# A hybrid attention and mLSTM block: attention products of the second half of the queries in another bank, six weight tiles, the bias table head by head, gate products in four column groups

## The chip, the cores and the metric

The kernel runs on one core of a Trainium2 chip. The metric is the device time of one execution in microseconds, 1434.75 us as the median of three runs before the change (1434.04 to 1437.02). A core has engines that work beside each other: TensorE (matrix products), VectorE, ScalarE and GpSimd (element-wise work), SyncE (it issues transfers), and 16 DMA engines. Each executes its own instructions in order; semaphores tie them together. The profile calls them PE, DVE, ACT, POOL and SP; PEld is TensorE's loading of weights.

## The reference

One layer over x, 1024 tokens by 1024 channels:

```python
xn = _rmsnorm(h, norm_w[layer])
(da_q, da_k, da_v, da_z, ml_q, ml_k, ml_v, ml_o, ml_z, ml_i, ml_f,
 gate_a, gate_m) = [xn @ wp for wp in _split_columns(w_in[layer])]
y_a = _diff_attention(da_q, da_k, da_v, lam[layer], subln_w[layer], rel_bias,
                      lambda_init) * jax.nn.silu(da_z)
y_m = _mlstm(ml_q, ml_k, ml_v, ml_i, ml_f, ml_o, ...) * jax.nn.silu(ml_z)
merged = g_a * (y_a @ w_pa[layer]) + g_m * (y_m @ w_pm[layer])
h = h + merged @ w_out[layer]
```

The attention has 8 heads. For each block of 128 queries:

```python
bias = rel_bias[_rel_bucket(kpos[None, :] - qpos[:, None])]
mask = (kpos[None, :] // CHUNK) <= (qpos[:, None] // CHUNK)
logits = jnp.einsum("pbhqd,pbhkd->pbhqk", qb, k).astype(jnp.float32) + bias
probs = jax.nn.softmax(jnp.where(mask, logits, NEG_INF), axis=-1)
attn = probs[0] - lam * probs[1]
return jnp.einsum("bhqk,bhkv->bhqv", attn, v)
```

so there are two softmaxes per head (p = 0 and 1), a bias that depends only on the distance of key and query, and a norm of each head's output. `ml_i` and `ml_f` are 16 columns of `w_in`, the gates of the mLSTM's eight heads.

## The kernel before

**Products.** Activations and weights are split into two float16 parts, and each float32 product is made of three (hi*hi, hi*lo, lo*hi: L329 to L331 with weights stationary, L358 to L360 with activations stationary). A unit is a set of 256 weight columns: it is loaded in two halves of 4 x 256 columns (L226, tiles `wt`, pool of `WT` = 3), squared on ScalarE for a common scale (L245, in `prep`), its scale is found by a short chain on VectorE with a TensorE sum in it (`fnorm_finish`, L165, L135 to L139), and it is split on ScalarE (L257) and VectorE (L259) into tiles `wp`. `prep` is a generator; the main loop takes one step of it with each step of the running unit's products.

**Start.** `normed` and `startup` bring x into the transposed, normalised, split form X (eight tiles, from transposes L396 read by ScalarE at L398 and VectorE at L399). `tables` is woven into the second half of it: it computes the differential factor, and the bias table `tb` (8 heads x 384 distances, a one-hot product), which L432 writes to memory for all heads at once, 128 copies of each row at a pitch of 513, so that a read with pitch 512 (`strip`, L584) yields each query's shifted row. The first unit of attention (`c_aqk(0)`, queries and keys of head 0) runs meanwhile, and `if_proj` makes the gates' 16 columns: `wifp` (32 columns, 16 hi and 16 lo) is stationary, 1024 tokens in two halves `th` stream by, and the sums over hi and lo parts of X are added up in one accumulation of 16 products for each half (L468).

**The order of phases.** `phases` lists groups of units, each with a side generator whose steps are put between the products: for seven groups `attention(h, PLAN_A)` of head h beside the units of head h + 1 (`aqk`, then `avz`), for the next `attention(7, PLAN_C)` beside the gate units, then the mLSTM heads. A plan entry (slot, name) puts a piece at a slot of the products' steps.

**One head's attention.** q_i is the product of query block i with all its keys for p = 0, r_i does the same for p = 1 and then combines and transposes (`both`); QK stands for these products (L812). They go to `psb`, one buffer of two banks, which VectorE reads with the bias strip in `BB` added and the maximum taken (L822); ScalarE makes the exponential (L826), VectorE combines the two softmaxes (L832 to L837), ScalarE and VectorE split the result (L844, L845) and a transposing DMA on SP (L847) turns it into z, the stationary operand of v_i (L855 to L857), the product with the values. v_0 to v_3 fill one bank of `pvp`, v_4 to v_7 the next buffer of that tag, and `pvp` has one buffer. f_k takes the factor of the output norm of four blocks on GpSimd (L862 to L864), o_k reads the bank with it on VectorE (L870), t_k transposes the result. The other small products and transposes take banks of the tag `pmi`, which has two buffers. `BB` is filled from the strip by VectorE at the start of each head (L800).

Of the kernel before, what the change touches and what calls it, by code (L numbers as in the profile page):

```python
# [48 lines left out]
def block_kernel(ctx, tc, x, norm_w, w_in, lam, subln_w, rel_bias, conv_w, conv_b, b_if,  # L49
# [355 lines left out]
    tb_d = dram.tile([H, P * 513], F32, tag="tbd", name="tb_d")  # L405

    def tables():
        oh = R(shape=[NB, 384], p="oh")
# [17 lines left out]
        tb_ps = m_ps()  # L426
        te.matmul(tb_ps[:H, :384], rb, oh, start=True, stop=True)
        tb = R(shape=[H, 384], p="tb")
        v.tensor_copy(tb, tb_ps[:H, :384])
        v.tensor_scalar(tb, tb, tb[:, 0:1], None, op0=ALU.subtract)  # L430

        nc.sync.dma_start(tb_d.rearrange("h (q u) -> h q u", u=513)[:, :, :384],  # L432
                    tb.unsqueeze(1).to_broadcast([H, P, 384]))
        yield
# [13 lines left out]
    gif_d = dram.tile([32, S], F32, tag="gifd", name="gif_d")  # L448

    def if_proj():  # L450
# [12 lines left out]
        t = R(shape=[32, S], p="gif")  # L463
        for th in range(2):
            gps = m_ps()
            for i in range(KC):
                for k in range(2):
                    te.matmul(gps[:32, :], parts[:, i, :], x_src(i, th)[k], start=(i + k == 0),  # L468
                              stop=(i + k == KC))
# [1 line left out]
            s.activation(t[:, HS[th]], gps[:32, :], AF.Copy, scale=sig[:32, :])
# [101 lines left out]
    def c_aqk(h, w):  # L573
# [10 lines left out]
        nc.sync.dma_start(strip, tb_d[h, :P * 512].rearrange("(q u) -> q u", u=512)[:, 127:383])  # L584
# [10 lines left out]
        def post(cb, th, ap):  # L595
# [7 lines left out]
            if done[cb] == 2:  # L603
                for p in range(2):
                    src = x2[p * 64:p * 64 + 64]
                    for j in range(2):
                        if cb == 0:
                            nc.sync.dma_start(Q[j * 64:j * 64 + 64, p, :], src[:, j, :])
                        else:
                            nc.sync.dma_start(K[p][j * 64:j * 64 + 64, :, :], src)  # L610
        return None, post
# [276 lines left out]
    def mlstm(h):  # L888
# [333 lines left out]
```

## Time and profile before

| | us |
|---|---|
| median of three runs | 1434.75 (1434.04 to 1437.02) |
| the profiled execution, its own time | 1435.78 |
| its span from first to last instruction | 1433.9 |
| TensorE busy | 1380.6 |
| VectorE busy | 848.0 |
| ScalarE busy | 735.0 |
| GpSimd busy | 157.5 |
| mean granted TensorE clock | 0.995 |

The profile records one execution. A row of a group names line, engine, operation, output <- inputs by the program's names, the count, busy time and the mean length of one; behind it stands the idle time of the engine just before such instructions and what ended most of it. A row of the timeline gives start and length, and in brackets the idle time before it and what ended that. TensorE's instructions overlap in the pipeline: one with 512 columns is shown with 380 ns, but the next starts 0.216 us later, with 256 columns 0.109 us later.

### The profile page before, as it was taken

Reading aid. Unit: us, or ns where it says so; the run is one execution under the profiler, and the core shown is the slowest. Engines: PE = TensorE matmul, PEld = TensorE weight load, DVE = VectorE, ACT = ScalarE, POOL = GpSimd, SP = SyncE. Lnnn points to the kernel's source line nnn. Section 1 sums busy time; section 2 is a strip of 40 time slices with the busy share of each in tenths; the row PEclk is TensorE's granted clock in tenths of the full one; section 3 lists DMA queues with packets and bytes.
Section 4 is the critical chain, followed back from the end, with each engine's and each line's share of the span. In section 5 each row is a group of like instructions: output and inputs, shape, how many; then the busy total and the mean of one; then the engine's idle time right before and its main releaser. Section 6 shows DMA issues by size and latency. Waiting matters only on the chain.

```text
span 1433.9 us, 25050 instructions
## 1 busy us (share of the span) xinstructions
PE 1380.6 (96%) x9650; PEld 913.3 (64%) x9650; DVE 848.0 (59%) x2310; ACT 735.0 (51%) x1533; POOL 157.5 (11%) x215
## 2 busy tenths in 40 slices
PE   6989999999999999999999999999999999999997
PEld 3656575665756655444486787778769675444786
DVE  6276868677686756533445674775866564233633
ACT  7276556565566667832353444443435344644542
POOL 2001010010100100100102020220211200122004
PEclk9999999999999999999999999999999999999999
DMA  6456355463554645543321313231232135534303
GB/s 200 68 142 140 83 107 124 104 141 82 114 121 91 136 95 130 163 149 125 96 74 60 104 31 101 47 87 47 66 97 75 60 86 158 168 103 162 118 16 118
DMA packets 232585, 150.14 MB, mean 105 GB/s; under 512 B 117297, under 2 KB 209730, under 8 KB 232466
## 3 DMA queue, kind: packets, MB, share of 16 engines
q1 hardware_dynamic: 218450, 123.28, 35.0%
q10 hardware_dynamic: 14016, 25.27, 5.3%
q8 instruction: 75, 1.23, 0.3%
q14 instruction: 44, 0.36, 0.1%
HBM read 90.12 MB, written 18.55 MB: 76 GB/s over the span
## 4 chain that ended last, share of the span: by engine, by line
PE 77%; DVE 9%; ACT 4%; DMA 4%; POOL 3%; issue 3%; SPq 0%; POOLq 0%; DVEq 0%; ACTq 0%
PE pp L329 14%; PE pp L331 14%; PE pp L330 14%; PE pp L360 8%; PE pp L358 8%; PE pp L359 8%; PE psb L812 3%; DVE z L822 3%; DMA z<-z 2%; ACT z L826 1%; DMA qw<-rows_d 1%; DVE wp L259 1%; PE psb L908 1%; PE pvp L855 1%; DVE hl L600 1%
## 5 line engine op out<-in xcount | busy, mean ns | idle before, releaser
L358 PE MATMUL pp<-wp,X 128*128 128x256 f16 x1280 | 349.7, 273 | 0.0
L359 PE MATMUL pp<-wp,X 128*128 128x256 f16 x1280 | 349.7, 273 | 0.0
L360 PE MATMUL pp<-wp,X 128*128 128x256 f16 x1280 | 349.7, 273 | 0.0
L329 PE MATMUL pp<-X,wp 128*128 128x512 f16 x768 | 291.7, 380 | 0.3 <-ACT wp L257 0.3
L331 PE MATMUL pp<-X,wp 128*128 128x512 f16 x768 | 291.3, 379 | 0.6 <-DVE wp L259 0.6
L330 PE MATMUL pp<-X,wp 128*128 128x512 f16 x768 | 291.8, 380 | 0.0
L257 ACT ACTIVATE wp<-wt,sb 128x512 f16<-128x512 f32 x208 | 136.9, 711 | 105.4 <-DVE sb L138 70.6
L331 PEld LDWEIGHTS <-wp 128*128 128x128 f16 x1024 | 100.0, 98 | 119.7 <-DVE wp L259 1.2
L245 ACT ACTIVATE junk<-wt 128x1024 bf16<-128x1024 f32 x112 | 118.1, 1055 | 100.0 <-DMA wt<-in_w_in_dram 89.7
L329 PEld LDWEIGHTS <-wp 128*128 128x128 f16 x1024 | 100.2, 98 | 103.0 <-issue 1.7
L330 PEld LDWEIGHTS <-wp 128*128 128x128 f16 x1024 | 100.1, 98 | 97.1
L259 DVE SCALAR_TENSOR_TENSOR wp<-wt,sb,wp 128x512 f16<-128x512 f32 x208 | 150.5, 760 | 14.4 <-ACT wp L257 12.8
L359 PEld LDWEIGHTS <-X 128*128 128x128 f16 x1280 | 125.3, 98 | 18.4 <-issue 2.4
L358 PEld LDWEIGHTS <-X 128*128 128x128 f16 x1280 | 125.4, 98 | 16.8 <-issue 0.8
L360 PEld LDWEIGHTS <-X 128*128 128x128 f16 x1280 | 125.3, 98 | 14.6
L826 ACT ACTIVATE z<-z,mx 128x256 f32<-128x256 f32 (+7 forms) x128 | 99.0, 773 | 61.7 <-DVE mx L825 46.1
L822 DVE CUSTOM_DVE_ANT_0 z<-psb,BB,negc 128x256 f32<-128x256 f32 (+7 forms) x128 | 104.1, 813 | 19.7 <-PE psb L812 19.4
L331 PE MATMUL pp<-Y,wp 128*128 128x512 f16 x256 | 97.1, 379 | 0.0
L330 PE MATMUL pp<-Y,wp 128*128 128x512 f16 x256 | 97.1, 379 | 0.0
L329 PE MATMUL pp<-Y,wp 128*128 128x512 f16 x256 | 97.1, 379 | 0.0
L649 DVE SCALAR_TENSOR_TENSOR acc<-up,wcol,acc 128x512 f32<-128x512 f32 x96 | 78.0, 827 | 27.4 <-POOL acc L650 24.5
L812 PE MATMUL psb<-K,Q 128*128 128x512 f16 (+3 forms) x384 | 83.5, 326 | 7.8 <-DMA K<-hl 4.6
(245 smaller groups left out, 2012.1 us busy)
## 6 DMA issues: line engine op xcount, KB each, us to landing
wt<-in_w_in_dram SPq DMA_DIRECT2D x128, 256.0 KB, 3.4
wt<-in_w_in_dram SPq DMA_DIRECT2D x24, 512.0 KB, 3.9
K<-hl SPq DMA_DIRECT2D x32, 256.0 KB, 3.7
gate_d<-tg ACTq DMA_DIRECT2D x32, 256.0 KB, 2.2
xt<-in_x_dram SPq DMA_DIRECT2D x8, 512.0 KB, 5.2
Q<-hl SPq DMA_DIRECT2D x32, 128.0 KB, 2.4
wt<-in_w_pa_dram SPq DMA_DIRECT2D x8, 512.0 KB, 5.4
ft<-gate_d ACTq DMA_DIRECT2D x16, 256.0 KB, 2.8
```

Source lines behind the costliest of these rows:

```text
L245: s.activation(j, w.wt[k], AF.Square, accum_out=ss[:, k:k + 1])
L257: s.activation(dst[0], src, AF.Copy, scale=w.sb)
L259: v.scalar_tensor_tensor(dst[1], src, w.sb, dst[0], op0=ALU.mult, op1=ALU.subtract)
L329: te.matmul(ps, wh, xh, start=(start and i == 0), stop=False, **kw)
L330: te.matmul(ps, wh, xl, start=False, stop=False, **kw)
L331: te.matmul(ps, wl, xh, start=False, stop=(stop and i == n - 1), **kw)
L358: te.matmul(ps[:, o], xh[:, t], wh, start=i == 0, stop=False)
L359: te.matmul(ps[:, o], xh[:, t], wl, start=False, stop=False)
L360: te.matmul(ps[:, o], xl[:, t], wh, start=False, stop=i == KC - 1)
L812: te.matmul(sp[:, c:e], Q[:, p, i * P:(i + 1) * P], K[p][:, j, c:e], start=(j == 0), stop=(j == 1))
L822: v.tensor_tensor_reduce(z[:, :n], sp[:, :n], bb[:, S - n:], negc, BIG, op0=ALU.add, op1=ALU.min, accum_out=mx)
L826: s.activation(z[:, :n], z[:, :n], AF.Exp, bias=mx, scale=-1.0, accum_out=rr[:, 2 * i + p:2 * i + p + 1])
```

## The change

The small products of the second half of the queries (v_4 to v_7) take a bank of the tag `pmi` instead of a new buffer of `pvp`, and `PLAN_A` puts v6, v7, f1 and o1 at other slots. The pool of weight tiles has six instead of three, the loads run one unit further ahead, and the third unit is loaded at the start. The bias table is written one head at a time on ScalarE's queue (`write_table`): head 0 from `tb` in a generator of its own (`first_table`), which also stores the 8 x 384 table, and each later head from that copy, a unit ahead of its use. The strip is read when the second column block of its unit is done (`bias_strip`), behind the issue of K, and the mask is made from the strip itself by one operation, without the constant `maskv`. The gate products of hi and lo and of the two halves go to four groups of 32 columns, in one bank of `psb`, issued in turn, and `if_gates` adds the parts up with two more loads and two more additions. The number of idle steps in `prep` becomes a parameter (5; 2 for the first unit), and the buffer `st` of the mLSTM has one copy.

The lists of `PLAN_A` are cut at their front:

```diff
-PLAN_A = [... (30, 'f0'), (30, 'o0'), (31, 'v6'), (31, 'v7'), (42, 't0'), (55, 'f1'), (55, 'o1'), (55, 't1')]
+PLAN_A = [... (30, 'f0'), (30, 'o0'), (33, 'v6'), (35, 'v7'), (42, 't0'), (43, 'f1'), (44, 'o1'), (55, 't1')]
-WT = 3
+WT = 6
...
+    s.dma_start(rb, rel_bias)
+    s.dma_start(oh, onehot)
...
+        for _ in range(slack):
+            yield
...
-    tb_d = dram.tile([H, P * 513], F32, tag="tbd", name="tb_d")
+    tb_d = [dram.tile([1, P * 513], F32, tag=f"tbd{h}", name=f"tb_d{h}") for h in range(H)]
+    tbr_d = dram.tile([H, 384], F32, tag="tbrd", name="tbr_d")
+
+    def write_table(h):
+
+        s.dma_start(tb_d[h].rearrange("h (q u) -> h q u", u=513)[:, :, :384],
+                    (tbr_d if h else tb)[h:h + 1].unsqueeze(1).to_broadcast([1, P, 384]))
+
+    def first_table():
+        for _ in range(3):
+            yield
+        tb_ps = m_ps()
+        te.matmul(tb_ps[:H, :384], rb, oh, start=True, stop=True)
+        tn0 = sm(p="tn0", bufs=1)
+        v.tensor_scalar(tn0[:H, :], tb_ps[:H, 0:1], -1.0, None, op0=ALU.mult)
+        s.activation(tb, tb_ps[:H, :384], AF.Identity, bias=tn0[:H, :])
+        yield
+        write_table(0)
+        s.dma_start(tbr_d, tb)
+        yield
 
...
-        nc.sync.dma_start(tb_d.rearrange("h (q u) -> h q u", u=513)[:, :, :384],
-                    tb.unsqueeze(1).to_broadcast([H, P, 384]))
...
-        t = R(shape=[32, S], p="gif")
-        for th in range(2):
-            gps = m_ps()
-            for i in range(KC):
+
+        t = R(shape=[P, 512], p="gif")
+        gps = s_ps()[:, :512]
+        for i in range(KC):
+            for th in range(2):
                 for k in range(2):
-                    te.matmul(gps[:32, :], parts[:, i, :], x_src(i, th)[k], start=(i + k == 0),
-                              stop=(i + k == KC))
-                yield
-            s.activation(t[:, HS[th]], gps[:32, :], AF.Copy, scale=sig[:32, :])
-        nc.sync.dma_start(gif_d, t)
+                    o = (th * 2 + k) * 32
+                    te.matmul(gps[o:o + 32, :], parts[:, i, :], x_src(i, th)[k], start=(i == 0), stop=(i == KC - 1))
+        yield
+        s.activation(t, gps, AF.Copy, scale=sig)
+        s.dma_start(gif_d, t)
...
+        for k, dst in ((0, gi), (1, ff), (2, gl[0]), (3, gl[1]), (4, gl[2]), (5, gl[3])):
+            r = k * H if k < 4 else 32 + (k - 4) * H
+            nc.sync.dma_start(dst.rearrange("h (t a) b -> h t (a b)", t=2),
+                              gif_d.rearrange("(t r) c -> r t c", t=2)[r:r + H])
...
+            v.tensor_tensor(dst, dst, gl[2 + k], op=ALU.add)
...
-        nc.sync.dma_start(strip, tb_d[h, :P * 512].rearrange("(q u) -> q u", u=512)[:, 127:383])
-        g.tensor_scalar(strip, strip, invc, 1.0, op0=ALU.mult, op1=ALU.mult)
         mc = sm(p="mc")
-        v.tensor_scalar(mc, invc, 2.0 ** 20, None, op0=ALU.min)
-        g.tensor_scalar(strip[0:64, 192:256], maskv, mc[0:64, :], 1.0, op0=ALU.mult, op1=ALU.mult)
+        v.tensor_scalar(mc, invc, 2.0 ** 20, -(2.0 ** 100), op0=ALU.min, op1=ALU.mult)
+        if h + 1 < H:
+            write_table(h + 1)
+
+        def bias_strip():
+            nc.sync.dma_start(strip, tb_d[h][0, :P * 512].rearrange("(q u) -> q u", u=512)[:, 127:383])
+            g.tensor_scalar(strip, strip, invc, 1.0, op0=ALU.mult, op1=ALU.mult)
+            masked = strip[0:64, 192:256]
+            g.tensor_scalar(masked, masked, 0.0, mc[0:64, :], op0=ALU.mult, op1=ALU.add)
...
+                if cb == 1:
+                    bias_strip()
...
-                ops[i // 4] = v_ps()
+                ops[i // 4] = m_ps() if i else v_ps()
...
+    order[2].finish_load()
...
-    weave(startup(1), tables())
+    weave(startup(1), tables(), first_table())
...
-                        pq[at + 1].start_load()
+                        pq[at + 1].finish_load()
+                    if at + 2 < len(pq):
+                        pq[at + 2].start_load()
```

What the scheduler makes of it is read from the order of the instructions. Numbers behind an underscore tell buffers apart; a line of after is that of before plus 1 to 21 (L329 to L331 are L330 to L332, L358 to L360 are L359 to L361, L812 is L833, L855 is L876, L870 is L891, L399 is L400); a bracket names the engines or DMA queues whose semaphores an instruction waits for.

First TensorE at v4 of head 2, before:

```order
L360 MATMUL pp_2844<-wp_2627,X_288 128x256
L358 LDWEIGHTS X_306
L358 MATMUL pp_2844<-wp_2642,X_306 128x256
L855 LDWEIGHTS z_2619 [waits DMAHW0_49]
L855 MATMUL pvp_2871<-vr_2064,z_2619 128x128 [waits DVE_49]
L856 LDWEIGHTS z_2619
```

and now:

```order
L360 MATMUL pp_2857<-wp_2646,X_271 128x256
L361 LDWEIGHTS X_271
L361 MATMUL pp_2857<-wp_2646,X_271 128x256
L876 LDWEIGHTS z_2628 [waits DMAHW7_49]
L876 MATMUL pmi_2884<-vr_2076,z_2628 128x128
L877 LDWEIGHTS z_2628
```

The product v4 goes to another bank, and its first matrix product waits for no engine any more, only its weight load for the transposed z. It stands 48 rows behind the head's last QK, with v3 among them; before it was 90, without v3.

Second TensorE where the QK of head 1 begin, at the end of head 0's phase. Before:

```order
L812 MATMUL psb_1697<-K_913,Q_912 128x128 [waits DMAHW0_49]
L812 LDWEIGHTS Q_912
L812 MATMUL psb_1697<-K_913,Q_912 128x128
L329 LDWEIGHTS wp_1474
L329 MATMUL pp_1689<-X_214,wp_1474 128x512
L330 LDWEIGHTS wp_1474
L330 MATMUL pp_1689<-X_214,wp_1474 128x512
L331 LDWEIGHTS wp_1474
L331 MATMUL pp_1689<-X_214,wp_1474 128x512
L812 LDWEIGHTS Q_912 [waits DMAHW3_49,DMAHW6_49,DMAHW4_49]
L812 MATMUL psb_1705<-K_914,Q_912 128x128 [waits DVE_49]
```

and now:

```order
L833 MATMUL psb_1714<-K_922,Q_920 128x128 [waits DVE_49]
L833 LDWEIGHTS Q_920
L833 MATMUL psb_1714<-K_922,Q_920 128x128
L833 LDWEIGHTS Q_920
L833 MATMUL psb_1727<-K_921,Q_920 128x256 [waits DVE_49]
L833 LDWEIGHTS Q_920
L833 MATMUL psb_1727<-K_921,Q_920 128x256
L833 LDWEIGHTS Q_920
L833 MATMUL psb_1755<-K_922,Q_920 128x256 [waits DVE_49]
L833 LDWEIGHTS Q_920
L833 MATMUL psb_1755<-K_922,Q_920 128x256
```

Between the QK of two softmaxes there were products of the running unit (`pp_1689`). They are gone; the QK follow each other, six pieces from QK 0 with p = 1 to QK 3 with p = 0, and behind them stands v7 of head 0.

Third VectorE in the loading phase, at the last quarter of X (`X_394` before, `X_408` now). Before:

```order
L399 SCALAR_TENSOR_TENSOR X_394<-pmi_395,nws_134,X_394 128x512 [waits Activation_49]
L600 SCALAR_TENSOR_TENSOR hl_535<-pp_497,hl_535 128x512 [waits Activation_49]
L135 TENSOR_SCALAR nb_438<-pmi_436 128x1 [waits PE_49]
L399 SCALAR_TENSOR_TENSOR X_394<-pmi_402,nws_134,X_394 128x512 [waits Activation_49]
L137 TENSOR_SCALAR nb_438<-nb_438 128x1 [waits DVE_49]
L135 TENSOR_SCALAR nb_484<-pmi_482 128x1 [waits PE_49]
```

and now:

```order
L596 SCALAR_TENSOR_TENSOR invc_914<-sigm_911 128x1 [waits DVE_49]
L591 SCALAR_TENSOR_TENSOR negc_909<-sig_906 128x1 [waits DVE_49]
L567 TENSOR_TENSOR sig_1295<-isb_1037,isx_123 128x1 [waits DVE_49]
L599 TENSOR_SCALAR mc_917<-invc_914 128x1 [waits DVE_49]
L572 TENSOR_SCALAR hs_1297<-sig_1295 128x1 [waits DVE_49]
L637 TENSOR_SCALAR isz_160<-sig_1295 128x1
L641 TENSOR_SCALAR eps_1302<-sig_1295 128x1
L642 TENSOR_TENSOR eps_1302<-eps_1302 128x1 [waits DVE_49]
L643 RECIPROCAL eps_1302<-eps_1302 128x1 [waits DVE_49]
L644 TENSOR_SCALAR eps_1302<-eps_1302 128x1 [waits DVE_49]
L400 SCALAR_TENSOR_TENSOR X_408<-pmi_416,nws_137,X_408 128x512 [waits Activation_49]
```

The last quarter stood behind one operation of the scale of the first prepared units; now behind two such chains for units that come later, and, further up, behind the copy of the strip into `BB`. On SP the loads of the third unit's weights, and the strips of heads 0 and 1, now stand ahead of the transfers of Q and K of head 0; before it was the strip of head 0 that stood among them.

More of the change, by code (lines that the diff above doesn't have):

```diff
@@ L35 @@
 RING = 15
-PLAN_A = [(0, 'q0'), (0, 'r0'), (0, 'q1'), (3, 'r1'), (4, 'q2'), (5, 'r2'), (9, 'q3'), (9, 'r3'), (9, 'q4'), (10, 'v0'), (14, 'v1'), (16, 'r4'), (17, 'q5'), (18, 'v2'), (19, 'r5'), (21, 'q6'), (24, 'r6'), (25, 'q7'), (27, 'r7'), (28, 'v3'), (29, 'v4'), (29, 'v5'), (30, 'f0'), (30, 'o0'), (31, 'v6'), (31, 'v7'), (42, 't0'), (55, 'f1'), (55, 'o1'), (55, 't1')]
+PLAN_A = [(0, 'q0'), (0, 'r0'), (0, 'q1'), (3, 'r1'), (4, 'q2'), (5, 'r2'), (9, 'q3'), (9, 'r3'), (9, 'q4'), (10, 'v0'), (14, 'v1'), (16, 'r4'), (17, 'q5'), (18, 'v2'), (19, 'r5'), (21, 'q6'), (24, 'r6'), (25, 'q7'), (27, 'r7'), (28, 'v3'), (29, 'v4'), (29, 'v5'), (30, 'f0'), (30, 'o0'), (33, 'v6'), (35, 'v7'), (42, 't0'), (43, 'f1'), (44, 'o1'), (55, 't1')]
 PLAN_C = [(0, 'q0'), (0, 'r0'), (6, 'q1'), (7, 'r1'), (7, 'q2'), (9, 'r2'), (16, 'q3'), (19, 'r3'), (19, 'q4'), (19, 'r4'), (19, 'v0'), (22, 'v1'), (22, 'v2'), (25, 'q5'), (28, 'r5'), (29, 'q6'), (31, 'v3'), (32, 'v4'), (33, 'r6'), (37, 'q7'), (38, 'f0'), (38, 'r7'), (46, 'o0'), (52, 'v5'), (52, 'v6'), (63, 'v7'), (64, 'f1'), (67, 'o1'), (82, 't1'), (83, 't0')]
@@ L117, in block_kernel @@
     g.memset(BB, 0.0)
-    maskv = ctile([64, 64], p="maskv")
-    g.memset(maskv, -(2.0 ** 100))
     xts = [R(p="xt") for _ in range(NT)]
@@ L125, in load_x @@
         nc.sync.dma_start(xts[tt], x[0, tt * P:(tt + 1) * P, :])
+    rb = ctile([NB, H], p="rb")
+    oh = R(shape=[NB, 384], p="oh")
+    tb = R(shape=[H, 384], p="tb")
+    s.dma_start(rb, rel_bias)
+    s.dma_start(oh, onehot)
     nrows = ctile([KC, P], p="nrows")
@@ L197, in block_kernel @@
     lamb = early[:, :256].rearrange("p (a b) -> p a b", a=4)
-    rb = ctile([NB, H], p="rb")
     def load_small():
         nc.sync.dma_start(lamb, lam.to_broadcast([P, 4, HD]))
-        nc.sync.dma_start(rb, rel_bias)
         nc.sync.dma_start(rows[0:64, :], conv_w[0].rearrange("g j (k p) -> (g j k) p", p=P))
@@ L232, in wparts, with prep @@
         return wpool.tile([P, 2] + shape, F16, tag="wp", name=nm("wp"), bufs=WP)
-    def prep(w, rowscale=None, keep=False):
+    def prep(w, rowscale=None, keep=False, slack=5):
         wd = w.width
@@ L246, in prep @@
             yield
-        yield
-        yield
+        for _ in range(slack):
+            yield
         w.sb = sm(p="sb")
@@ L313, in start_prep @@
                 self.finish_load()
-                self.prepping = prep(self.w, self.rowscale and self.rowscale(), self.keep)
+                self.prepping = prep(self.w, self.rowscale and self.rowscale(), self.keep, 2 if self is first else 5)
                 self.left = 16
@@ L404, in block_kernel @@
     lnc = ctile([P, 1], p="lnc")
-    tb_d = dram.tile([H, P * 513], F32, tag="tbd", name="tb_d")
+    tb_d = [dram.tile([1, P * 513], F32, tag=f"tbd{h}", name=f"tb_d{h}") for h in range(H)]
[15 more added lines that the diff above has]
+        yield
     def tables():
-        oh = R(shape=[NB, 384], p="oh")
-        nc.sync.dma_start(oh, onehot)
         lj = R(shape=[P, HD], p="lj")
@@ L425, in tables @@
         yield
[L426 to L432, printed above, removed]
-                    tb.unsqueeze(1).to_broadcast([H, P, 384]))
-        yield
         cols_ps = m_ps()
@@ L447, in block_kernel @@
     wsc = ctile([P, NT, H], p="wsc")
-    gif_d = dram.tile([32, S], F32, tag="gifd", name="gif_d")
+    gif_d = dram.tile([P, 512], F32, tag="gifd", name="gif_d")
     def if_proj():
@@ L477, in if_gates @@
         ff = R(shape=[H, NT, P], p="ff")
-        gl = [R(shape=[H, NT, P], p="gl") for _ in range(2)]
-        for k, dst in ((0, gi), (1, ff), (2, gl[0]), (3, gl[1])):
-            nc.sync.dma_start(dst.rearrange("h a b -> h (a b)"), gif_d[k * H:k * H + H, :])
+        gl = [R(shape=[H, NT, P], p="gl") for _ in range(4)]
+        for k, dst in ((0, gi), (1, ff), (2, gl[0]), (3, gl[1]), (4, gl[2]), (5, gl[3])):
+            r = k * H if k < 4 else 32 + (k - 4) * H
+            nc.sync.dma_start(dst.rearrange("h (t a) b -> h t (a b)", t=2),
+                              gif_d.rearrange("(t r) c -> r t c", t=2)[r:r + H])
         for _ in range(4):
@@ L919, in mlstm @@
         num = R(shape=[P, NT, P + 1], p="num")
-        st = sm(cols=48, p="st", bufs=2)
+        st = sm(cols=48, p="st", bufs=1)
         mv = sm(cols=16, p="mv", bufs=2).rearrange("p (c k) -> p c k", k=2)
```

1 line of the change is left out of this document (removed).

## The prediction

> **What bounds the kernel now.** The page first, for the share of each engine; then the busy time in stretches (columns: TensorE, weight loads, VectorE, ScalarE, GpSimd, granted clock, DMA share, GB/s); then TensorE's waits.
>
> ```profile
> PE 1380.6 (96%) x9650; PEld 913.3 (64%) x9650; DVE 848.0 (59%) x2310; ACT 735.0 (51%) x1533; POOL 157.5 (11%) x215
> ...
> 0.00:20.00 20.00, 8.07 (x25) 4.10 (x25) 10.32 (x35) 12.49 (x21) 7.09 (x24) 1.00 0.94 300
> ...
> 60.00:80.00 20.00, 14.93 (x134) 12.91 (x133) 5.30 (x22) 7.47 (x14) 0.78 (x2) 0.89 0.71 146
> ...
> 100.00:560.00 460.00, 437.51 (x3322) 286.83 (x3321) 336.98 (x936) 291.08 (x654) 33.20 (x57) 1.00 0.53 113
> 560.00:1340.00 780.00, 778.93 (x5101) 504.52 (x5100) 418.21 (x1108) 349.74 (x672) 97.38 (x103) 1.00 0.34 101
> ```
>
> TensorE is the bound, with 1433.9 - 1380.6 = 53.3 us of idle time in all. The change adds and removes no TensorE work, save that small products may overlap; so a gain can only come out of those 53 us and out of half-clock time. They lie in the loading phase (11.9 before 20 us), in one hole between 60 and 80 us (5.1, at a mean clock of 0.89), and in the eight attention heads (22.5 between 100 and 560 us). From 560 to 1340 us TensorE stands still for 1.1 us: nothing is to be won there, only lost. What it waits for:
>
> ```profile
> PE pvp L855 <- DVE on L870: 12.0, 8, 1.6
> ...
> PE psb L812 <- DMA K<-hl: 4.6, 2, 2.5
> PE pvp L855 <- DMA z<-z: 4.2, 5, 1.1
> ```
>
> Once in each head the fifth small product (v4) waits 1.0 to 1.6 us for the reading of the bank that it reuses, and in five heads the last one (v7) waits for its transposed operand. The edits aim at these two stretches.
>
> **The hole at 74 us: the bias table.** TensorE's rows, VectorE's and the queue's, in order of time:
>
> ```profile
> 73.46 0.27 PE L360 MATMUL pp<-wp,X 128*128 128x256 f16 x1
> 74.23 0.16 PE L165 MATMUL pmi<-s,ones 128*128 128x1 bf16 x1 [0.50 <-ACT gif L471]
> 76.86 0.37 PE L812 MATMUL psb<-K,Q 128*128 128x128 f16 x2 [2.47 <-DMA K<-hl]
> 79.34 0.37 PE L812 MATMUL psb<-K,Q 128*128 128x128 f16 x2 [2.10 <-DMA K<-hl]
> 79.50 0.42 PE L358 MATMUL pp<-wp,X 128*128 128x256 f16 x1
> 79.72 0.42 PE L359 MATMUL pp<-wp,X 128*128 128x256 f16 x1
> ```
>
> ```profile
> L432 SPq DMA_DIRECT2D tb_d<-tb x1: 817/817/817, 34.5 to 34.5; - x1
> ```
>
> ```profile
> 69.22 0.35 SPq L584 DMA_DIRECT2D strip<-tb_d  x1
> 69.67 2.21 SPq L608 DMA_DIRECT2D Q<-hl  x3
> 71.93 3.20 SPq L610 DMA_DIRECT2D K<-hl  x4
> ```
>
> ```profile
> 36.00:50.00 14.00, 13.83 (x73) 6.91 (x71) 9.38 (x29) 6.77 (x12) 0.00 (x0) 1.00 0.49 58
> 50.00:68.50 18.50, 18.50 (x135) 12.77 (x133) 0.69 (x1) 0.60 (x1) 0.00 (x0) 1.00 0.50 59
> ```
>
> The table of all heads (1536 KB) is issued at 34.5 and holds half of the DMA engines until 68.5, some 32.5 us from 36. Only then does the strip leave the queue, and behind it stand Q and K of head 0. So K lands at 76.8 and TensorE has the 5.1 us hole. After it the rows at 79.50 and 79.72 stand 0.21 apart instead of 0.109: half clock, until about 82.5, costs 1.5 more. With one head's table at a time (an eighth of the bytes, 4 us at the old rate) the strip lands near 45 and K near 63, 9 us before it is needed: **+6.6 us** (bounds 3, if part of the hole stays, and 6.6).
>
> By the Trainium skill, "TensorE: Matmul & The Clock Gate", Part 1, about 3.4 us of idling halve the clock; the trace agrees (granted 0.50 from 76 to 82), and the price above is from the rows alone.
>
> **The gate products.** Before:
>
> ```profile
> L468 PE MATMUL pmi<-X,wifp x32: 378/379/388, 50.8 to 57.5; 128*32 128x512 f16 x32
> ```
>
> 32 products in 6.9 us, 0.2157 apart. Afterwards they go to four column groups of 32 in turn. If four run at once that is 8 x 0.2157 = 1.7 us. No row of before shows column groups; the bounds are 0 (the instructions stay the same in number and size, so a loss is unlikely) and 5.1 us of gain. I take 2.3 us for the whole, near the short end, because the four write different partitions of one bank and none waits for another, with a third on top for the 32 weight loads: **+4.6**. The Trainium skill, same page, Part 3, "Measured speedup vs the span model", gives 2.38 times for three column tiles of 512 and 3.07 for four row tiles; by 3.07 the gain would be 4.6. It also says that a weight load overlaps running products only where the row group differs, which speaks against it here, since all four use all rows; that is a rival below.
>
> **New waits at the start.** The order of VectorE now has 22 one-column operations (two chains of scale factors, and the copy of the strip) ahead of the last quarter of the normalised input X, which the first products need at once. What such a chain and such a quarter take:
>
> ```profile
> 74.49 0.15 DVE L135 TENSOR_SCALAR nb<-pmi 128x1 int32<-128x1 int32 x1
> ...
> 75.78 0.15 DVE L582 SCALAR_TENSOR_TENSOR invc<-sigm 128x1 f32<-128x1 f32 x1
> ```
>
> ```profile
> 41.50 0.74 DVE L399 SCALAR_TENSOR_TENSOR X<-pmi,nws,X 128x512 f16<-128x512 f32 x1
> ```
>
> Ten small ones and a larger one (0.33) fill 1.3 us, so 0.1 each; 22 are 2.2, the quarter 0.74, the way from TensorE 0.3: 3.2 us, less 0.6 us of products that stand between. **-2.7** (bounds 0, if the chain starts early, and -4.5).
>
> Then four query-key products (QK) of head 0 stand back to back, where products of the next projection stood between them. They share one bank, so each waits until VectorE has read the last one:
>
> ```profile
> L822 DVE CUSTOM_DVE_ANT_0 z<-psb,BB,negc 128x384 f32<-128x384 f32 x16 | 9.8, 614 | 2.7 <-PE psb L812 2.7
> ...
> L822 DVE CUSTOM_DVE_ANT_0 z<-psb,BB,negc 128x256 f32<-128x256 f32 x16 | 7.7, 482 | 4.0 <-PE psb L812 3.9
> ...
> L822 DVE CUSTOM_DVE_ANT_0 z<-psb,BB,negc 128x128 f32<-128x128 f32 x16 | 5.6, 348 | 0.0
> ```
>
> ```profile
> 77.27 0.35 DVE L822 CUSTOM_DVE_ANT_0 z<-psb,BB,negc 128x128 f32<-128x128 f32 x1
> ```
>
> From product (76.86) to reading (77.27) is 0.4, the reading 0.35 to 0.61, about 0.1 back: 0.85 to 1.1 a round. Four rounds to the next filler, 3.2 us, less their own 0.65: **-2.5** (bounds -1 and -3.5). Up to here +6.6 + 4.6 - 2.7 - 2.5 = +6.0.
>
> **Head 0 into head 1.** The order has six QK of head 1 (128 to 512 columns) back to back there, then v7 of head 0, then the first projection products that need freshly split weights. Five rounds of 0.85, 1.1, 1.1, 1.3, 1.3 less 1.2 of work are 4.5 us idle, the weights about 1. Before, the two stretches
>
> ```profile
> 100.00:124.00 24.00, 22.07 (x147) 12.93 (x146) 20.27 (x48) 14.99 (x32) 2.06 (x3) 1.00 0.65 140
> 124.00:146.00 22.00, 20.58 (x222) 18.22 (x222) 11.82 (x32) 12.92 (x29) 2.60 (x5) 1.00 0.62 130
> ```
>
> hold 1.9 + 1.4 = 3.3 us, which go with the bank. **-2.2** (bounds 0 and -5).
>
> **The second bank, in a steady head.** Head 1's end, as it is now:
>
> ```profile
> 178.08 1.02 PE L812 MATMUL psb<-K,Q 128*128 128x512 f16 x4
> ...
> 183.51 0.20 POOL L864 TENSOR_TENSOR fac<-fac,rc 128x4 f32<-128x4 f32 x1
> 183.75 0.61 DVE L870 SCALAR_TENSOR_TENSOR on<-pvp,fac,tz 128x128 f32<-128x128 f32 x2 [1.53 <-POOL fac L864]
> ...
> 184.34 0.33 DVE L870 SCALAR_TENSOR_TENSOR on<-pvp,fac,tz 128x128 f32<-128x128 f32 x1
> ...
> 185.12 0.22 PE L855 MATMUL pvp<-vr,z 128*128 128x128 f16 x1 [1.59 <-DVE on L870]
> ```
>
> ```profile
> L845 DVE TENSOR_TENSOR z<-z,z x1: 1226/1226/1226, 187.6 to 187.6; 128x1024 f16<-128x1024 f32 x1
> ```
>
> ```profile
> 193.86 0.23 PE L855 MATMUL pvp<-vr,z 128*128 128x128 f16 x1 [0.98 <-DMA z<-z]
> ```
>
> The wait of 1.59 goes: v4 writes a bank of its own. What is late next is v7. The last QK ends at 178.08 + 4 x 0.2157 = 178.94; its softmax chain ends at 188.8 and the transposed operand is there at 193.86, **14.9 us after the QK**, with 12.1 us of TensorE work between. VectorE still waits for the factor (1.53) ahead of this chain, but two of the four bank readings (0.33 each) now stand behind the chain's next step: 14.25. The new order has 12.4 us of work there, so v7 waits 1.85, against 1.59 + 0.98 before: **+0.75 a head**, for heads 1 to 5 +3.8 (bounds 0, and 2.6 a head). In head 6 (v4 waits 1.0 and v7 not at all) +0.5, in head 7 +1.4, since its v7 waits for nothing before.
>
> **Costed at nothing:** six weight tiles and loads a unit earlier (TensorE waits for no weight load now; three more squarings on ScalarE, 1.24 us each, lie before 45 us beside TensorE's work, at most -2); the two further loads and additions of the gates, under 1.3 us each by a 1024-column VectorE operation, while VectorE is 54% busy from 560 us; the shorter mask.
>
> **Sum.** +6.0 - 2.2 + 3.8 + 0.5 + 1.4 = +9.5. The profiled execution took 1435.78 (span 1433.9 and 1.9 around it), 1.0 above the median of 1434.75; 1435.8 - 9.5 - 1.0 gives **1425 us**.
>
> **Rivals.**
> 1. *The column groups run one after another*: the change doesn't do what it says there, 4.6 us less: 1430. For it: one moving path, weights loaded 32 times. Chance 0.14.
> 2. *All attention waits go*: v7 finds its operand, because the chain starts earlier than I make it. 1.85 x 6 = 11 us more: 1414. For it: 12.0 + 4.2 us of waits stand in the list. Against: the chain's 14.9 is the same in each head. Chance 0.12.
> 3. *Waits only change places*: nothing gained in heads 1 to 5 (v7 takes it all) and 5 us lost at head 0: 1425 + 3.8 + 2.8 = 1432. Chance 0.16.
> 4. *Slower: one head's table goes through one DMA engine.* Before, eight rows of heads kept 0.49 x 16 = 8 engines busy for 32.5 us, so each may have carried one head. A single head, from a single partition, would then still take 32.5 us: written at 68, strip at 72, copied at 73. VectorE stands before that copy with X behind it, so TensorE waits from 50 to 74, at least 20 us, against the 2.7 counted; the loss decides as soon as the strip lands after about 60. 1425 + 19 = 1444. The Trainium skill, "DMA: Bandwidth & Descriptors", "Why a DMA increments its semaphore by 16 and not by 1", says that the engines used are the largest number up to 16 that divides the slowest dimension longer than one; this agrees with the 8 of before, and would make it 16 for 128 rows. Chance 0.06, and 0.04 for other losses.
>
> The forecast has 0.48. A measurement of this kernel tells 0.2% (2.9 us) from no change. Faster: the forecast, rivals 1 and 2 and half of 3, 0.82; within 0.2%: 0.10; slower 0.08. The range takes in rival 1, 3 and most of 2: 1412 to 1435.
>
> **What the profile would show.** Right: no hole at 74, clock 1.00 there; the 32 gate products within 2.5 us; no wait for `on` at L876, but 1.5 to 2 us for z in each head; idle rounds of QK near 120 us; a short wait for X near 50. Wrong: gate products 0.2 apart; strip landing after 60 us; v7 without a wait; or TensorE idle after 560 us, for which I count nothing.

## The result and the profile after

The changed kernel takes 1454.9 us in the median, 1.26% more than before (ratio 1.0126, 95% interval 1.0111 to 1.0140), where 1425 was forecast with a range to 1435. One of its four runs, 2419.65 us at a granted clock of 0.559, is left out of the ratio. The profiled execution took 1455.34 us, its span is 1453.5. The page's first line and the stretches that answer to those of before (the same columns):

```profile
PE 1384.1 (95%) x9650; PEld 914.5 (63%) x9650; DVE 844.2 (58%) x2311; ACT 733.6 (50%) x1533; POOL 162.6 (11%) x214
...
0.00:20.00 20.00, 6.93 (x22) 3.60 (x23) 9.11 (x33) 11.55 (x19) 7.00 (x21) 1.00 0.93 299
...
40.00:60.00 20.00, 16.60 (x93) 7.12 (x95) 12.47 (x56) 9.91 (x17) 1.58 (x4) 0.85 0.47 54
60.00:80.00 20.00, 18.52 (x168) 15.51 (x161) 5.01 (x17) 5.76 (x14) 0.00 (x0) 0.98 0.78 194
...
560.00:1340.00 780.00, 765.70 (x5016) 497.23 (x5015) 404.40 (x1087) 342.45 (x654) 98.44 (x102) 1.00 0.34 96
```

TensorE's work is the same; what grew is its idle time. Between 60 and 80 us it shrank from 5.1 to 1.5 us, as meant. But a new hole stands before 60 us, with the clock at 0.85, and from 560 to 1340 us, where TensorE had stood for 1.1 us, it now stands for 14.3. TensorE's waits, after:

```profile
PE pmi L876 <- DMA z<-z: 9.7, 9, 1.8
PE psb L833 <- DVE mx L843: 9.1, 17, 1.3
...
PE psb L968 <- DVE C L951: 5.7, 7, 0.9
PE psb L966 <- ACT num L972: 4.8, 4, 1.8
```

The 12.0 us for `on` are gone. The wait for z has grown, as forecast. The last two rows are of the mLSTM heads, where nothing had been expected.

All these kernels execute the same 7680 projection products into `pp`, and from the 95th on in the same sequence. So the start of the product that stands behind n others, less its start in the kernel before, tells where time is lost (us, from the traces of the profiled executions; "+" is behind; the last row is the last product). Small products can be moved past a mark, so the marks stand where their order is alike:

| mark: n, the start before | what lies ahead of it | after | u_loads | u_slack | c_three | c_six | b_slack | a_nosq |
|---|---|---|---|---|---|---|---|---|
| 96, 57.8 | start, gate products | +2.7 | -2.7 | +0.3 | -2.1 | +1.1 | +4.3 | +2.9 |
| 288, 86.3 | the hole at 74 us | -1.8 | -3.6 | -4.4 | -5.6 | -3.6 | +2.9 | -1.6 |
| 768, 197.3 | heads 0 and 1 | +2.4 | -0.1 | +0.3 | -4.5 | -0.3 | +0.7 | +2.6 |
| 2208, 499.3 | heads 2 to 6 | +0.4 | -6.4 | +0.4 | -7.9 | -0.3 | -4.6 | +0.5 |
| 2496, 566.0 | head 7 | +4.0 | -6.9 | +4.9 | -7.6 | +5.7 | -4.7 | +4.3 |
| 3456, 745.8 | units before the mLSTM heads | +4.0 | -6.8 | +4.9 | -7.6 | +5.7 | -4.7 | +4.3 |
| 6400, 1228.1 | mLSTM heads | +19.8 | +8.6 | +3.8 | -8.4 | +4.6 | +14.8 | +8.3 |
| 7679, 1424.1 | the rest | +19.7 | +8.4 | +3.9 | -8.2 | +4.7 | +14.6 | +8.2 |

The column "after" has 15.8 of its 19.7 us in the mLSTM heads. The other columns are the experiments below.

### The profile page after: what moved, and what is told of

Same layout as the page of the kernel before. It is cut to its first block, busy times and chain, and to the rows that moved or that the text cites. A ratio compares the mean times of both kernels' runs of the same rounds, so it can differ in the third digit from the quotient of the medians.

```text
span 1453.5 us, 25019 instructions
## 1 busy us (share of the span) xinstructions
PE 1384.1 (95%) x9650; PEld 914.5 (63%) x9650; DVE 844.2 (58%) x2311; ACT 733.6 (50%) x1533; POOL 162.6 (11%) x214
## 3 DMA queue, kind: packets, MB, share of 16 engines
q8 instruction: 75, 1.23, 0.4%
## 4 chain that ended last, share of the span: by engine, by line
PE 66%; DVE 10%; issue 7%; ACT 6%; DMA 6%; POOL 3%; SPq 0%; POOLq 0%; DVEq 0%; ACTq 0%
PE pp L330 12%; PE pp L331 12%; PE pp L332 12%; PE pp L359 8%; PE pp L361 8%; PE pp L360 8%; DMA z<-z 4%; PE psb L833 3%; DVE acc L670 2%; DVE z L843 2%; ACT z L847 1%; ACT wp L258 1%; POOL acc L671 1%; DMA qw<-rows_d 1%; ACT junk L246 1%
## 5 line engine op out<-in xcount | busy, mean ns | idle before, releaser
L359 PE MATMUL pp<-wp,X 128*128 128x256 f16 x1280 | 349.0, 273 | 0.3 <-DVE tz L578 0.3
L360 PE MATMUL pp<-wp,X 128*128 128x256 f16 x1280 | 348.9, 273 | 0.0
L361 PE MATMUL pp<-wp,X 128*128 128x256 f16 x1280 | 348.9, 273 | 0.0
L331 PE MATMUL pp<-X,wp 128*128 128x512 f16 x768 | 293.3, 382 | 2.1 <-DVE X L400 2.1
L332 PE MATMUL pp<-X,wp 128*128 128x512 f16 x768 | 293.0, 382 | 0.6 <-DVE wp L260 0.6
L330 PE MATMUL pp<-X,wp 128*128 128x512 f16 x768 | 292.9, 382 | 0.3 <-ACT wp L258 0.3
L332 PEld LDWEIGHTS <-wp 128*128 128x128 f16 x1024 | 100.5, 98 | 122.6 <-issue 4.7
L330 PEld LDWEIGHTS <-wp 128*128 128x128 f16 x1024 | 100.5, 98 | 104.0 <-issue 3.1
L331 PEld LDWEIGHTS <-wp 128*128 128x128 f16 x1024 | 100.5, 98 | 99.7 <-issue 2.0
L260 DVE SCALAR_TENSOR_TENSOR wp<-wt,sb,wp 128x512 f16<-128x512 f32 x208 | 146.9, 750 | 13.3 <-ACT wp L258 12.3
L360 PEld LDWEIGHTS <-X 128*128 128x128 f16 x1280 | 125.2, 98 | 16.9 <-issue 1.0
L359 PEld LDWEIGHTS <-X 128*128 128x128 f16 x1280 | 125.3, 98 | 16.7 <-issue 0.8
L361 PEld LDWEIGHTS <-X 128*128 128x128 f16 x1280 | 125.3, 98 | 15.2
L332 PE MATMUL pp<-Y,wp 128*128 128x512 f16 x256 | 97.0, 379 | 0.0
L331 PE MATMUL pp<-Y,wp 128*128 128x512 f16 x256 | 97.0, 379 | 0.0
L330 PE MATMUL pp<-Y,wp 128*128 128x512 f16 x256 | 97.0, 379 | 0.0
L833 PE MATMUL psb<-K,Q 128*128 128x512 f16 (+3 forms) x384 | 83.9, 327 | 9.6 <-DVE mx L843 9.1
```

Of the source, the lines that this page charges most:

```text
L260: v.scalar_tensor_tensor(dst[1], src, w.sb, dst[0], op0=ALU.mult, op1=ALU.subtract)
L330: te.matmul(ps, wh, xh, start=(start and i == 0), stop=False, **kw)
L331: te.matmul(ps, wh, xl, start=False, stop=False, **kw)
L332: te.matmul(ps, wl, xh, start=False, stop=(stop and i == n - 1), **kw)
L359: te.matmul(ps[:, o], xh[:, t], wh, start=i == 0, stop=False)
L360: te.matmul(ps[:, o], xh[:, t], wl, start=False, stop=False)
```

## The experiments

**What makes the loss in the mLSTM heads.** In one of these heads ScalarE's rows are, before and after (start, length, idle time before):

```profile
771.70 1.06 ACT L245 ACTIVATE junk<-wt 128x1024 bf16<-128x1024 f32 x1 [0.42 <-DMA wt<-in_w_in_dram]
...
774.16 1.06 ACT L245 ACTIVATE junk<-wt 128x1024 bf16<-128x1024 f32 x1 [1.31 <-DMA wt<-in_w_in_dram]
...
775.69 0.49 ACT L951 ACTIVATE num<-psb 128x387 f32<-128x387 f32 x1 [0.38 <-PE psb L947]
```

```profile
778.78 1.06 ACT L246 ACTIVATE junk<-wt 128x1024 bf16<-128x1024 f32 x1 [3.15 <-DMA wt<-in_w_in_dram]
...
781.74 1.06 ACT L246 ACTIVATE junk<-wt 128x1024 bf16<-128x1024 f32 x1 [1.81 <-DMA wt<-in_w_in_dram]
...
782.80 0.47 ACT L972 ACTIVATE num<-psb 128x387 f32<-128x387 f32 x1
```

and TensorE's, after:

```profile
783.33 0.49 PE L966 MATMUL psb<-vr,E 128*128 128x129 f32 x2 [1.54 <-ACT num L972]
```

The copy `num`, which empties TensorE's bank, used to wait for TensorE (0.38). Now it stands behind two squarings of later weights that wait for their loads, starts with no wait of its own the moment they end, and TensorE waits for it. The wait for `C` (L951), the larger of the two in the list, comes the same way by a detour. In the next head ScalarE's copy `up`, for the convolution, starts with no wait of its own the moment the second squaring ends; GpSimd's sum waits for it, VectorE for that sum, and `C` stands behind on VectorE:

```profile
833.13 0.58 ACT L346 ACTIVATE up<-pp 128x512 f32<-128x512 f32 x1
```

```profile
834.61 0.75 DVE L670 SCALAR_TENSOR_TENSOR acc<-up,wcol,acc 128x512 f32<-128x512 f32 x1 [7.12 <-POOL acc L671]
...
837.08 0.34 DVE L951 SCALAR_TENSOR_TENSOR C<-C,decb,pmi 128x129 f32<-128x129 f32 x1
```

Before, the same copy waited for its product:

```profile
823.92 0.60 ACT L345 ACTIVATE up<-pp 128x512 f32<-128x512 f32 x1 [1.10 <-PE pp L331]
```

Three parts of the change could put the squarings there, and each was undone alone; the second bank was undone too.

u_loads:

```diff
-WT = 6
+WT = 3
-    order[2].finish_load()
...
-                        pq[at + 1].finish_load()
-                    if at + 2 < len(pq):
-                        pq[at + 2].start_load()
+                        pq[at + 1].start_load()
```

> The changed kernel with three weight tiles instead of six, loads one unit ahead as before, and no load of the third unit at the start; all else as changed. Theory A (the loads further ahead put two squarings, each waiting for its weight load, ahead of the copies of the mLSTM on ScalarE): TensorE's idle time between the start of the mLSTM heads and the last of them falls from about 16 us to 1 or 2, and the whole takes 1436 to 1440. Theory B (the longer pause in prep, five steps for two, moves the splits onto the mLSTM's copies): no change, 1450 to 1455. Theory C (one buffer of st serialises two heads): no change either.

u_slack:

```diff
-                self.prepping = prep(self.w, self.rowscale and self.rowscale(), self.keep, 2 if self is first else 5)
+                self.prepping = prep(self.w, self.rowscale and self.rowscale(), self.keep, 2)
```

> The changed kernel with two idle steps in prep for every unit, as before; all else as changed. Theory A: the mLSTM heads keep at least 12 of their 16 us, 1448 to 1455. Theory B: they lose them, 1436 to 1440. Theory C: no change.

u_st:

```diff
-        st = sm(cols=48, p="st", bufs=1)
+        st = sm(cols=48, p="st", bufs=2)
```

> The changed kernel with two buffers of st, as before; all else as changed. Theories A and B: within 2 us of the changed kernel, 1450 to 1455. Theory C: 12 us or more are won in the mLSTM heads.

u_pv:

```diff
-                ops[i // 4] = m_ps() if i else v_ps()
+                ops[i // 4] = v_ps()
```

with the old `PLAN_A`.

> The changed kernel with v4 to v7 in a new buffer of pvp and the old PLAN_A; all else as changed. If the second bank is worth what its trace says (heads 2 to 6 from 4.7 to 0.4 us behind the kernel before, so some 4 us won, and 3.5 lost in head 7), the whole is 0 to 3 us slower than the changed kernel; if the crowding of QK at head 0 and 1 comes from the plan, it is 3 to 6 us faster; the mLSTM heads stay as they are in both cases.

| | median, us | ratio to before (95%) |
|---|---|---|
| u_loads | 1445.2 | 1.0069 (1.0053 to 1.0086) |
| u_slack | 1440.9 | 1.0037 (1.0024 to 1.0050) |
| u_st | 1456.3 | 1.0151 (1.0134 to 1.0168) |
| u_pv | 1460.6 | 1.0177 (1.0161 to 1.0192) |

u_loads came out between what the theories expected: without the earlier loads and the six tiles the mLSTM heads lose as much as with them (-6.8 to +8.6), so theory A fell for these heads, but 11 us are won ahead of them. Theory B held: with the old pause these heads lose nothing (+4.9 to +3.8), and 1440.9 is just above its 1436 to 1440. Theory C fell. Undoing the second bank with its plan costs 5.7 us more, beyond the 0 to 3 expected, so it isn't the culprit, nor is it in head 7: by the trace of u_pv that head loses 8.2 us without the bank, against 3.6 with it.

Then the pause was made alone in the kernel before (five idle steps where there were two, for the first unit too), and in the changed kernel the squarings of the mLSTM's units were taken out.

b_slack:

```diff
-    def prep(w, rowscale=None, keep=False):
+    def prep(w, rowscale=None, keep=False, slack=5):
...
-        yield
-        yield
+        for _ in range(slack):
+            yield
...
-                self.prepping = prep(self.w, self.rowscale and self.rowscale(), self.keep)
+                self.prepping = prep(self.w, self.rowscale and self.rowscale(), self.keep, 5)
```

> The kernel before with five idle steps in prep for two, alone. If the pause by itself makes the loss of the mLSTM heads (theory B), these heads are 12 to 16 us longer, with little change in the attention: 1447 to 1452. If it needs the other parts: within 3 us of before.

a_nosq:

```diff
+        w.ml = unit.kind in ('mqk', 'mvo', 'mz')
...
+        if w.ml:
+            g.memset(ss, 1.0)
         for k in range(2):
-            j = junk(4 * wd).rearrange("p (a b) -> p a b", a=4)
-            s.activation(j, w.wt[k], AF.Square, accum_out=ss[:, k:k + 1])
+            if not w.ml:
+                j = junk(4 * wd).rearrange("p (a b) -> p a b", a=4)
+                s.activation(j, w.wt[k], AF.Square, accum_out=ss[:, k:k + 1])
             yield
```

> The changed kernel without the squaring of the weights on ScalarE in the mLSTM units; the scale of these units comes from a constant. Mechanism 1 (five idle steps put the splits, so the release of the weight tiles, so the next loads, 2 us later; the squarings that wait for these loads then stand ahead of the copies for which TensorE waits): 12 us or more of the 16 are gone, 1436 to 1441. Mechanism 2 (the splits themselves collide with the pieces of the mLSTM, and the squarings have no part): at least 12 of the 16 stay, 1447 to 1453.

The stretch of 780 us over these heads, of b_slack and of u_slack:

```profile
560.00:1340.00 780.00, 765.29 (x4979) 495.95 (x4978) 404.62 (x1087) 342.32 (x657) 97.03 (x102) 1.00 0.33 96
```

```profile
570.00:1350.00 780.00, 779.40 (x5102) 506.52 (x5100) 418.85 (x1120) 349.64 (x670) 94.52 (x101) 1.00 0.34 100
```

The pause alone (1448.4, ratio 1.0087, 1.0065 to 1.0109) makes 14.7 us of idle time there, and by the table these heads lose 19.5 us; in the changed kernel with the old pause 0.6 us of idle time are left. That the whole came out within the 1447 to 1452 expected is luck: the heads lost more than the 12 to 16, the start lost 4.3, and the attention, where little change was expected, won 7.6 (+2.9 to -4.7). So the pause isn't bad everywhere. Without the squarings (1441.7, ratio 1.0044, just above the 1436 to 1441 expected) the same copy is on time:

```profile
779.99 0.49 ACT L976 ACTIVATE num<-psb 128x387 f32<-128x387 f32 x1 [4.03 <-PE psb L972]
```

and the loss over these heads falls from 15.8 to 4.0 us, all of it in the last two heads; there the gate units, whose squarings were kept, are prepared and run beside the last one. So the way is shown: three more idle steps put the splits later (the first one of the head above from 764.7 to 772.6, now behind 18 more projection products), the splits give the weight tiles back later, the next loads are issued later (from 767.9 to 774.8) and land later (the squarings moved from 771.7 and 774.2 to 778.8 and 781.7, while the products around them moved by 4 us), and in ScalarE's fixed order the copies stand behind them.

**What makes the loss in the attention.** Both undone together, and then the parts of the loading apart, always with the old pause and with the other parts of the change:

c_three (u_loads and u_slack together):

> The changed kernel with both undone: three weight tiles and the old loads, and two idle steps in prep. If the pause made the loss in the mLSTM heads (16 us) and the loads ahead made that of the attention (11 us), and neither needs the other, then the trace follows the run without the loads up to 566 us (6.9 us ahead of the kernel before) and gains or loses under 1 us from there: 1428 to 1430. If the mLSTM loss was from the pause only in the presence of six tiles, or the attention's from both together, it stays above 1433.

c_wt (six tiles, loads further ahead; against c_three):

```diff
-WT = 3
+WT = 6
...
-                        pq[at + 1].start_load()
+                        pq[at + 1].finish_load()
+                    if at + 2 < len(pq):
+                        pq[at + 2].start_load()
```

> Six weight tiles and the loads one unit further ahead, with the other parts of the change, two idle steps in prep, and no load of the third unit at the start. Without tiles and loads it was 1428.8, with them and the third unit's load 1440.9. If the loads ahead make the 12 us: 1438 to 1442. If the third unit, prepared beside the start, makes them: 1428 to 1431.

c_early (six tiles, third unit at the start; against c_three):

```diff
-WT = 3
+WT = 6
...
+    order[2].finish_load()
```

> Six weight tiles and the third unit's load at the start, the loads otherwise one unit ahead as before, with the other parts of the change and two idle steps in prep. If the third unit's load makes the 12 us, 1438 to 1442; if the loads ahead make them, 1428 to 1431.

c_six (against c_three):

```diff
-WT = 3
+WT = 6
```

> Six weight tiles alone added to the run with three (1428.8): loads one unit ahead as before, no third unit at the start, two idle steps. If the number of tiles by itself lets the squarings and the scales of later units come early and stand in the way (X near 50 us, the passage from head 0 to 1, head 7): 1438 to 1442, as with either of the loads. If the tiles cost nothing without the earlier loads: 1428 to 1431.

| | median, us | ratio to before (95%) |
|---|---|---|
| c_three | 1428.8 | 0.9951 (0.9939 to 0.9964) |
| c_wt | 1441.9 | 1.0042 (1.0027 to 1.0057) |
| c_early | 1440.1 | 1.0037 (1.0023 to 1.0050) |
| c_six | 1440.2 | 1.0036 (1.0024 to 1.0049) |

Neither load is needed: the number of tiles alone costs 11.4 us (13.0 between the two traces). With tiles free, the squarings of later units (eight in all start before 42 us, five in c_three) and the scale chains behind them come early, ahead of what is needed now. VectorE at the last quarter of X, in c_three and in c_six:

```profile
50.07 1.40 DVE L400 SCALAR_TENSOR_TENSOR X<-pmi,nws,X 128x512 f16<-128x512 f32 x2
51.39 0.14 DVE L138 TENSOR_SCALAR nb<-pmi 128x1 int32<-128x1 int32 x1
```

```profile
51.06 0.16 DVE L138 TENSOR_SCALAR nb<-pmi 128x1 int32<-128x1 int32 x1
...
52.74 0.15 DVE L644 TENSOR_SCALAR eps<-eps 128x1 f32<-128x1 f32 x1
52.81 0.74 DVE L400 SCALAR_TENSOR_TENSOR X<-pmi,nws,X 128x512 f16<-128x512 f32 x1
```

The chains now stand ahead of X. And in head 7, ScalarE and TensorE's waits of c_six:

```profile
563.11 0.51 ACT L241 ACTIVATE wt<-wt,fa 128x256 f32<-128x256 f32 x1 [4.76 <-DMA wt<-in_w_pa_dram]
563.52 1.04 ACT L865 ACTIVATE z<-z 128x1024 f16<-128x1024 f32 x1
```

```profile
PE pmi L876 <- ACT junk L879: 2.7, 1, 2.7
```

The scaling of a later unit's weights waits 4.8 us for its load, and the last softmax's split (L865) and the copy `junk` (L879, at 566.67) stand behind it; TensorE's last product waits 2.7 us for `junk`. In c_three that split starts at 551.89, with no such load ahead of it. It is the mLSTM's mechanism again, and 5.8 of the 13.0 us. Another 5.6 us arise in heads 0 to 2, in several waits of 1 to 2 us; they weren't taken apart, so for them the way is not shown.

**The parts that the prediction had priced, each alone on the kernel before.**

b_pv:

> The kernel before with the second bank for v4 to v7 and the new PLAN_A alone. My sum had 0.75 us a head and 1.9 us for heads 6 and 7, less 2.2 at the passage from head 0 to 1: about 3.5 us faster, 1431 to 1433. The rival, that all the waits of v4 go and nothing takes their place: 12 us, 1423 to 1425. The other, that the wait for z takes it all: 1435 to 1437.

b_gates:

> The kernel before with the gate products in four column groups alone, with its loads and additions. If four run at once at full clock, 32 products take 1.7 to 2.3 us in place of 6.9, and 4.6 to 5.1 us are won, 1430 to 1431.5, unless the hole at 74 us takes it: it is set by the transfers of K behind the bias table, which do not start earlier, so that then nothing is won, 1434 to 1436. I take the second.

b_table:

> The kernel before with the bias table written head by head and the strip read later, alone. The hole at 74 us and the half clock behind it (6.6 us) go; QK of head 0 may stand back to back (2.5 us back): 1429 to 1433. If one head's table is as slow as the whole was (32 us), TensorE waits from about 60 us on and it is slower, 1445 or more.

| | median, us | ratio to before (95%) |
|---|---|---|
| b_pv | 1430.7 | 0.9966 (0.9953 to 0.9978) |
| b_gates | 1435.0 | 0.9997 (0.9988 to 1.0006) |
| b_table | 1446.3 | 1.0076 (1.0063 to 1.0088) |

b_pv won a little more than expected (4.8 us for some 3.5). b_gates is 5.4 us ahead behind the gate products and level again behind the hole at 74 us, which waits for transfers. b_table was a miss on both counts. The table is in time (its strip leaves at 46.9), yet from product 96 to 288, where the hole was, only 1.7 us are won, and head 0 loses 10.4 (to product 768). There TensorE waits up to 4.3 us for z and 3.5 for `on`. Ahead of that, VectorE stands at a later unit's scale, with the softmax of head 0 behind it:

```profile
100.12 0.16 DVE L138 TENSOR_SCALAR nb<-pmi 128x1 int32<-128x1 int32 x1 [4.24 <-PE pmi L168]
```

That loss isn't there when the three parts come together (c_three). That this one row makes the whole loss is not shown, and why the order falls out so with this part alone was not followed further.

**The pause only where attention runs.** c_sel (against c_three):

```diff
-                self.prepping = prep(self.w, self.rowscale and self.rowscale(), self.keep, 2)
+                self.prepping = prep(self.w, self.rowscale and self.rowscale(), self.keep, 5 if self is not first and self.kind in ('aqk', 'avz', 'ga') else 2)
```

> The run with three weight tiles (1428.8), with five idle steps for the units of attention and of its gates, except the first, and two for the others. The run with five steps everywhere and three tiles was 1.3 us better between 86 and 566 us of the kernel before, and 2 us worse before it: 1427 to 1431, no loss in the mLSTM heads. If the loss there comes in with the attention's units, 1436 or more.

1432.3 (ratio 0.9973, 0.9963 to 0.9982), above the 1427 to 1431 expected: no loss in the mLSTM heads, but against c_three 4.4 us are lost between the products 2496 and 3456, where TensorE waits once, 2.7 us, for the sum of a next unit's scale, and 2.5 ahead of them. The best version is c_three, faster than both kernels.

## Why the prediction was wrong, step by step

**The step that failed** is the one that costed edits "at nothing": "six weight tiles and loads a unit earlier (TensorE waits for no weight load now; ...)", together with the pause in `prep`, which the change's text names and the sum left out without a reason. What covered the tiles and loads was that TensorE waits for no weight load now, and a bound of 2 us for three more squarings ahead of 45 us. That looks at TensorE and at ScalarE's busy time, and neither covers: ScalarE is half idle, but it executes in order, and a squaring that waits for a load holds up the copy behind it. The pause costs 15.8 us in the mLSTM heads by the trace (14.0 in the medians, after against u_slack), the six tiles 11.4 us ahead of them. Connected with it is what the prediction says of 560 to 1340 us, "nothing is to be won there, only lost", which was right, and for which no loss was then counted. Of its own signs of being wrong this one came: TensorE is idle after 560 us.

**The hole at 74 us**: +6.6 less 2.5 for the QK behind it, so +4.1; from product 96 to 288 the trace of after shows 4.5, that of c_three 3.5. Right in these; b_table alone shows 1.7. The waits between the QK, 2.5 forecast, are 1.5 us in after and 2.9 in c_three. The table itself took longer than counted: 9 us, not 4. The prediction also has the clock halved by 3.4 us of idling; here it fell sooner. In the kernel before half the clock is granted from 75.8 to 82.6 us, and TensorE had worked up to 73.7, and then for one sum of 0.16 us. **The gate products**: 2.3 us forecast. They took, in c_three and after,

```profile
L479 PE MATMUL psb<-X,wifp x32: 379/379/391, 53.9 to 55.4; 128*32 128x512 f16 x32
```

```profile
57.04 3.60 PE L479 MATMUL psb<-X,wifp 128*32 128x512 f16 x32
```

1.7 us at full clock, 6.9 / 1.7 = 4 times as fast as before, so four do run at once (rival 1 fell), and 3.6 in the changed kernel. The Trainium skill, "TensorE: Matmul & The Clock Gate", Part 3, has 3.07 times for four row tiles and lets a weight load overlap only with another row group. For four column groups, with a weight load for each of the 32 products, the trace shows the 4 times above, and the measurement decides. **The wait for X**: 2.7 forecast; TensorE waits

```profile
52.50 0.16 PE L168 MATMUL pmi<-s,ones 128*128 128x1 bf16 x1 [1.23 <-DVE nb L138]
...
55.24 0.59 PE L331 MATMUL pp<-X,wp 128*128 128x512 f16 x1 [2.12 <-DVE X L400]
```

1.23 + 2.12 = 3.35, the first for a scale chain and the second for X. The wait was of about that size, but its sequel was missed: the clock is granted at 0.50 from 54 to 61 us, the products behind the wait are shown with 0.59 to 0.63 instead of 0.38, and all gate products fall in that time. In c_three, where the waits are shorter (1.10 and 0.26), the clock stays at 1.00, and behind the gate products it is 2.1 us ahead, for 4.6 - 2.7 = 1.9 forecast. The first product of after was 1.1 late besides.

**Head 0 into head 1**: 2.2 lost forecast, with 0.75 won in head 1; from 288 to 768 after lost 4.2, c_three 1.1, for 1.45 forecast. The QK do crowd, and most of the surplus came with the tiles. **The steady heads**: the wait for v4 went, and v7 waits instead, as forecast; heads 2 to 6 won 2.0 in the changed kernel and 3.4 in c_three, for 3.5 forecast. With the short pause another wait takes the place, though: in b_pv

```profile
PE pmi L165 <- DVE s L159: 8.8, 7, 1.6
```

the sum for the next unit's scale; with the long pause of after it is 0.3. **Head 7**: +1.4 forecast, 3.6 lost, and that from the tiles; but the 1.4 don't come without them either (c_three and b_pv lose 0.2 to 0.3 there).

**The other rivals**: "all attention waits go" fell (b_pv alone won 4.8 us, not 16). "Waits only change places" fell with c_three. The rival on the slower side had the wrong mechanism: the table of head 0 was issued at 39.0 and its strip could leave at 48.0, so not the 32 us of one engine. (Its price is off in its own terms, too: 20 less 2.7 is 17.3, not 19; and four rounds of 0.85 to 1.1 are 3.4 to 4.4, where the sum for the QK has 3.2. Neither decides anything.) The three priced parts together gave 6.7 us (c_three, median against median) where the sum had 9.5, so the sum was right within a third, and in the trace of c_three each stretch but head 7 comes within 1 us of its forecast. Each alone, though, they gave 4.8, 0.5 and -10.8: they aren't worth their terms by themselves.

## What to carry to other kernels

Price an edit that only moves or frees preparation by the in-order queue it lands in: list which instruction with a wait on a transfer then stands ahead of which step that the bound engine needs, stage by stage, however idle that engine is on average. More buffers and longer pauses weren't neutral here, where a scheduler decides the order: buffers let work come early and stand in the way, and the pause moved the release of buffers and all loads behind it, to a gain in the attention (7.6 us) and a greater loss in the mLSTM heads (19.5, both in b_slack). Change such settings one at a time; here two of them hid 6.7 us of gain under 26 us of loss (1454.9 against 1428.8).

## What was not expected of the hardware

One head's table, 192 KB as 128 copies of one row, was not in memory for 9 us when its source was a single row on chip (issued at 39.0; the strip, whose wait of 16.2 us is put down to this table, left at 48.0; in c_three and b_table it is 9.0 us as well), with the DMA engines up to 0.89 busy at 28 GB/s (the stretch by engines of the changed kernel, its last two columns):

```profile
42.00:45.00 3.00, 3.00 (x15) 1.37 (x14) 1.35 (x2) 1.76 (x4) 0.00 (x0) 1.00 0.89 28
```

The list of DMA issues of the same kernel (size, median us from issue to landing) has the same bytes from memory, for a later head:

```profile
tb_d<-tbr_d ACTq DMA_DIRECT2D x1, 192.0 KB, 3.7
```

They landed 3.7 us behind their issue. That the single row is the reason is the likely reading; no run changed it alone.
